# First recurrence of a hybrid decoder layer: scores packed as squares of 32 tokens

## The chip, the cores and the metric

The kernel runs on one core of a Trainium2 chip. A core has TensorE (matmul, with its own queue), VectorE (DVE), ScalarE (ACT), GpSimd (POOL) and a queue engine SyncE (SP) that only issues DMAs. The metric is the device time of one execution in microseconds.

## The reference

One decoder layer on 512 tokens of 1024 channels: a gated feed-forward part, a mixer with two recurrences, a second feed-forward part, each with a residual, and a last norm. All numbers are float32. The change touches the first recurrence (HGRN2, 8 heads of 128 channels):

```python
def hgrn2_chunked(q, k, v, log_f):
    """S_t = diag(f_t) S_{t-1} + k_t^T v_t (k_t = 1 - f_t), o_t = S_t^T q_t."""
    ...
        inter = jnp.einsum('bhtk,bhkv->bhtv', q_c * jnp.exp(b_c), S)
        diff = b_c[:, :, :, None, :] - b_c[:, :, None, :, :]
        decay = jnp.exp(jnp.where(causal, diff, -jnp.inf))
        scores = jnp.einsum('bhtk,bhsk,bhtsk->bhts', q_c, k_c, decay)
        intra = jnp.einsum('bhts,bhsv->bhtv', scores, v_c)
```

The score of a query token t and a key token s is a sum over channels of query, key and the product of all gates between s and t, zero for s > t.

## The kernel before

Matmul operands of the dense projections are split in two halves (a rounded `hi` and a rest `lo`), and `mm3` (lines 188 to 191) issues three matmuls per operand pair into one accumulator. The weights come in slabs of 512 columns through SP's queue; ScalarE casts the `hi` half (line 1754) and VectorE subtracts the `lo` half (line 1756), into three rotating pairs of buffers. The two feed-forward parts (`ffn`) stand before and after the mixer.

The mixer (`mixer`) has one thread (a Python generator) for each piece of work. A planner, `Desk` (lines 64 to 138), runs all threads in a simulated time and decides, engine by engine, in which order their instructions are recorded; the order on the chip is that order. A thread says `yield "use", engine, cost` before it issues (`V`, `A` and `T_`, lines 761 to 763, are the costs of VectorE, ScalarE and TensorE), `yield "get", tag, n` and `D.put` for places in a pool, `yield "on", event` and `D.fire` for events. The rank of a thread breaks ties. The thread `product` (rank 9) issues the dense projections in the order of `DENSE` and then `closing`, the projection of the second recurrence's output: 16 operand pairs `so[k]` for each of 8 output blocks, in quarters, those of blocks 0 and 1 taking turns.

The first recurrence is `h_head(i)`, one thread per head, in chunks of 128 tokens (`NT` = 4 of them). It never divides by a gate. It builds the 128 x 128 scores of a chunk, keys in partitions, queries in columns, by levels hh = 1, 2, 4 ... 64: at level hh the tokens form pairs of blocks of hh; the queries of a pair's second block meet the keys of its first one, after `qp` and `ke` were multiplied by the gates in between (line 988 on VectorE, `keys` at line 929 on GpSimd). Its steps, with their lines:

- 909 to 912: `qp` is the query times its gate; `qq` holds, per chunk, the 128 queries and beside them the 64 odd columns of `qp`.
- 913 to 920: the opening product `pd`: 4 matmuls, one per chunk, 128 keys against 192 columns, into two PSUM banks. Its diagonal is the score of a token with itself, and its last 64 columns are level 1.
- 921 to 925: the score tile `at` (name `ah`, two buffers of the pool `on`) gets the 128 columns of `pd` times the identity, so its diagonal and zeros elsewhere.
- 956 to 961: level 1, two masked copies (`copy_predicated` with the mask `hm`).
- 963 to 975: levels 2 to 16, `pl`: per chunk and square of 32 tokens one matmul of 32 keys against the 16 queries of second blocks, 16 matmuls per head and level. The two heads of a pair meet before each level ("at" events), so that their blocks stand together.
- 932 to 941 (`fill`): masked copies into the score tile, one for each of the four squares of 32 partitions, four per level.
- 942 to 946: levels 32 and 64 are copied by ScalarE.
- 1014 to 1037: `po`, scores times values plus queries times state, and the state's update, chunk after chunk.

The second recurrence (`g_e`, `g_n`, `g_b`, `g_inv`, `g_w`, `g_rec`, eight pairs of heads u) runs mostly after the first. Its triangular inverse starts on GpSimd (lines 1236 to 1241) from an identity that is loaded from `hmask` (line 1234). The outputs of the last pair, u = 7, go from two transposes (line 1445, `pto`) through VectorE (1449), ScalarE (1458) and VectorE (1460) into `so[14]` and `so[15]`, which the first quarter of `closing` that needs them reads.

Of the kernel before, what the change touches and what calls it, by code (L numbers as in the profile page):

```python
# [16 lines left out]
P = 128  # L17
T = 512
NT = T // P
# [118 lines left out]
        assert not self.asked, [(th.rank, th.want) for th in self.asked]  # L138


def body(tc, xT, cst, sqc, hmask, dta, w1o, w1a, w2a, wt, wn, wab, wbh, wbg, wo, w1b, w2b, yT, dbg=None):
    nc = tc.nc
    pe, act, dve, pool, sp = nc.tensor, nc.scalar, nc.vector, nc.gpsimd, nc.sync
    ctx = ExitStack()
# [12 lines left out]
    cs = cp.tile([P, 256], F32, name="cs")  # L157
    sq = cp.tile([P, 3, P], F32, name="sq")
    ident, tri, strict = sq[:, 0], sq[:, 1], sq[:, 2]
    hm = cp.tile([P, 5, 64], F32, name="hm")  # L160
    dtab = cp.tile([P, 32], F32, name="dtab")[:16, :2]
    ones = cp.tile([P, P], F32, name="ones")
    dve.memset(ones, 1.0)
# [451 lines left out]
        return pts, lambda: products(KD - 1, {1: spread})  # L615

    def lead():
        sp.dma_start(hm, hmask[:, 0:5])
        sp.dma_start(dtab, dta)

    def last(go, pl, units, on, hooks):
# [66 lines left out]
def mixer(tc, mp, e):  # L688
# [29 lines left out]

    places = {}
    for size, names in ((1024, "n2:2 gz:2 fs:1 ut:1"), (512, "kn:3 gm:1 qm:2 gb:2 ln:1 at:4 vb:4 t64:2 on:2"),  # L720
                        (256, "ft:1 tp:1 thg:2 x:1 we:1 s:3 w:1"), (128, "fm:1"), (64, "sm:4")):
        for it in names.split():
            n, b = it.split(":")
            places[n] = alloc(n, int(b))

    hv = h.rearrange("p (a b) t -> p a (b t)", a=4)
    eye4 = e["hmask"][:, 5:9].rearrange("p a (i c) -> p (a i) c", c=8)


    lb0, lb1 = cs[:, C_LB:C_LB + 8], cs[:, C_LB + 8:C_LB + 16]  # L730
# [26 lines left out]


    D = Desk(wx0=1, wx1=1, wx2=1, wx3=1, mm=2, a=2, b=2, d=1, e=1, ta=TA, tm=6, thg=1, raw=RB, w=WB, n2=2, gz=2, fs=1, ut=1, t=3, kn=3, gm=1,
             qm=2, gb=2, ln=1, mi=3, mt=3, at=4, vb=4, t64=2, on=2, ft=1, x=1, we=1, w_=1, s=3)  # L760
    V = lambda n: ("use", "DVE", 0.21 + 0.001 * n)
    A = lambda n: ("use", "ACT", 0.2 + 0.0009 * n)
    T_ = lambda n: ("use", "PE", n)
# [4 lines left out]
    def place(tag, name, shape, n):  # L768

        taken[tag] = taken.get(tag, 0) + 1  # L770
        if taken[tag] == n:
            D.fire(("free", tag))
        return places[tag](name, shape)
# [82 lines left out]
    def h_q(i, pt):  # L856
        yield "get", "ta", 2
        yield "on", "rbc"
        yield *V(512), 1
        qs = ta("qs")  # L860
        dve.tensor_tensor(qs, pt, rbc, op=ALU.mult)
        D.put("mm")
        yield A(512)
        th = ta("th")
        act.activation(th, qs, AF.Tanh, scale=0.5)
        tag = ("fs", "ut")[i % 2]
        yield "get", tag, 1
        yield V(512)
        qq = hq[i] = place(tag, "qq", (P, NT, 192), 4)
        dve.scalar_tensor_tensor(qq[:, :, :P], v3(th, NT), 1.0, v3(qs, NT), op0=ALU.add, op1=ALU.mult)  # L870
        D.put("ta", 2)
        D.fire(("Q", i))

# [28 lines left out]
    def h_head(i):  # L902
# [3 lines left out]
        yield "get", "gb", 1  # L906
        yield V(512)
        qp = place("gb", "qp", (P, T), 8)
        dve.tensor_tensor(v3(qp, NT), qq[:, :, :P], v3(f, NT), op=ALU.mult)
        q4 = qp.rearrange("p (c g b) -> p c g b", c=NT, b=2)  # L910
        yield V(256)
        dve.tensor_copy(qq[:, :, P:192], q4[:, :, :, 1])
        yield "get", ln_, 2
        yield T_(1.32)
        pd = [ps("pd", ln_), ps("pd2", ln_)]
        for c in range(NT):
            pe.matmul(pd[c // 2][:, (c % 2) * 192:(c % 2) * 192 + 192], ke[:, c * P:(c + 1) * P], qq[:, c],  # L917
                      start=True, stop=True)
        D.put(tag_q)
        D.fire(("pd", i))  # L920
        yield "get", "on", 1
        at = place("on", "ah", (P, NT, P), 8)
        for q in range(2):
            yield V(256)
            dve.tensor_tensor(at[:, 2 * q:2 * q + 2], v3(pd[q][:, :384], 2)[:, :, :P], mid(ident, 2), op=ALU.mult)

        def keys(li, kv, fv, hh):
            yield "use", "POOL", .88
# [2 lines left out]

        def fill(li, hh, pl_):
            if hh <= 16:
                a5 = at.rearrange("p c (r g two b) -> p c r g two b", r=4, two=2, b=hh)
                for r in range(4):
                    rows = slice(32 * r, 32 * r + 32)
                    yield V(60)
                    dve.copy_predicated(a5[rows, :, r, :, 1],
                                        v3(hm[rows, li, 16 * r:16 * r + 16].bitcast(I32), 16 // hh).unsqueeze(1)
                                        .to_broadcast([32, NT, 16 // hh, hh]),  # L940
                                        pl_[rows, :NT * 16].rearrange("p (c g b) -> p c g b", c=NT, b=hh))
            else:
                for b in range(64 // hh):
                    s0 = 2 * b * hh
                    yield A(4 * hh)
                    act.copy(at[s0:s0 + hh, :, s0 + hh:s0 + 2 * hh], v3(pl_[s0:s0 + hh, :NT * hh], NT))
            D.put(ln_)
            D.fire(("full", i, li))

        fl, held = f, "at"  # L950
        for li, hh in enumerate((1, 2, 4, 8, 16, 32, 64)):
            n2 = T // (2 * hh)
            av = at.rearrange("p c (g two b) -> p c g two b", two=2, b=hh)
            if li:
                yield "on", ("ke", i, li - 1)
            if hh == 1:
                for q in range(2):
                    yield V(240)
                    dve.copy_predicated(av[:, 2 * q:2 * q + 2, :, 1, 0], mid(hm[:, li].bitcast(I32), 2),
                                        v3(pd[q][:, :384], 2)[:, :, P:192])  # L960
                D.put(ln_, 2)
            else:
                yield "get", ln_, 1
                D.fire(("at", i, li))
                yield "on", ("at", i ^ 1, li)
                yield T_(.6 if hh <= 16 else .5)
                pl_ = ps("pl", ln_)
                if hh <= 16:

                    qv = qp.rearrange("p (c r g two b) -> p c r g two b", c=NT, r=4, two=2, b=hh)  # L970
                    for c in range(NT):
                        for r in range(4):
                            s0 = 32 * r
                            pe.matmul(pl_[s0:s0 + 32, c * 16:(c + 1) * 16], ke[:, c * P + s0:c * P + s0 + 32],  # L974
                                      qv[:, c, r, :, 1], start=True, stop=True)
                else:
                    for c in range(NT):
                        for b in range(64 // hh):
                            s0 = 2 * b * hh
                            pe.matmul(pl_[s0:s0 + hh, c * hh:(c + 1) * hh], ke[:, c * P + s0:c * P + s0 + hh],  # L980
                                      qp[:, c * P + s0 + hh:c * P + s0 + 2 * hh], start=True, stop=True)
                D.start((2, i, 1), fill(li, hh, pl_))
            fv = fl.rearrange("p (g two) -> p g two", two=2)
            qv = qp.rearrange("p (g two b) -> p g two b", two=2, b=hh)
            kv = ke.rearrange("p (g two b) -> p g two b", two=2, b=hh)
            D.start((2, i), keys(li, kv, fv, hh))
            yield V(270)
            dve.tensor_tensor(qv[:, :, 1], qv[:, :, 1], bc(fv[:, :, 0], hh), op=ALU.mult)
            tag = ("x", "we")[i % 2] if hh == 1 else ("w", "ft")[i % 2] if hh == 2 else "tm"
            yield "get", "w_" if tag == "w" else tag, 1  # L990
            yield V(min(n2, 200))
            fn = tm(f"fl{hh}", (P, n2)) if tag == "tm" else place(tag, f"fl{hh}", (P, n2), 4)
            dve.tensor_tensor(fn, fv[:, :, 0], fv[:, :, 1], op=ALU.mult)
            yield "on", ("ke", i, li)
            D.put(held)
            if hh == 1:
                D.fire(("L", i))
            fl, held = fn, "w_" if tag == "w" else tag
# [18 lines left out]
        for c in range(NT):  # L1017
# [5 lines left out]
            pe.matmul(o, at[:, c], v[:, c, hs], start=True, stop=c == 0)  # L1023
            if c > 0:
                pe.matmul(o, qp[:, c * P:(c + 1) * P], s, start=False, stop=True)
            if c < NT - 1:
                pu = ps("pu", "b")
                pe.matmul(pu[:, :P], kn[:, c], v[:, c, hs], start=True, stop=True)
# [829 lines left out]
    D.start((0,), norm())  # L1858
    D.start((3, -1), loader())
    D.start((9,), product())  # L1860
    for i in range(8):
        D.start((2, i), h_head(i))
    for i in range(4):
# [58 lines left out]
def layout(i):  # L1922
# [8 lines left out]
        conv.reshape(4, 32, P).transpose(2, 1, 0).reshape(P, 128)], axis=1)  # L1931
    a = np.arange(P)
    sqc = np.stack([np.eye(P), a[:, None] <= a[None, :], a[None, :] < a[:, None]], 1)
    hmask = np.zeros((P, 9, 64))
    for l, hh in enumerate(LEVELS):
        g, b = np.divmod(np.arange(64), hh)
        hmask[:, l] = (a[:, None] >= 2 * hh * g) & (a[:, None] < 2 * hh * g + hh)
    eye4 = np.eye(32).reshape(32, 8, 4).transpose(2, 0, 1)
    hmask[:, 5:] = np.tile(np.repeat(eye4, 8, axis=0), (4, 1, 1)).reshape(P, 4, 64)
    w_in = f["w_in"][0]  # L1940
    off = np.cumsum([0, 1024, 1024, 1024, 1024, 1024, 1024, 2048, 16, 16, 2048, 1024, 1024])
    part = [w_in[:, off[j]:off[j + 1]] for j in range(12)]
# [7 lines left out]
    def ffn(n):  # L1950
# [3 lines left out]
    w1a, w2a = ffn(1)  # L1954
    w1b, w2b = ffn(2)
    out = dict(
        xT=_kpn(x.T), cst=cst, sqc=sqc, hmask=hmask,
        dta=np.stack([f["gdn_dt_bias"][0], f["gdn_a_log"][0]], 1),
        w1o=w1a[ORDER[0]:ORDER[0] + 2].reshape(4, P, KD, P).transpose(2, 1, 0, 3).reshape(KD, P, 512),
        w1a=w1a, w2a=w2a, wt=wt, wn=wn, wab=_kpn(wab).reshape(P, -1),  # L1960
# [18 lines left out]
```

## Time and profile before

| | us |
|---|---|
| median of 3 runs | 1606.91 |
| lowest, highest run | 1606.55, 1606.93 |
| span of the profiled execution | 1604.7 |
| TensorE busy in it | 1593.7 |
| VectorE busy | 1145.7 |
| ScalarE busy | 831.0 |
| GpSimd busy | 408.8 |

The profile is of one execution; its span runs from the first to the last instruction, so the time of a run is a little longer. In its rows, PE is TensorE's matmul and PEld its weight load, L917 is line 917 of the kernel, `pd<-qq,ke` names the output and the inputs, `128*32` the rows and columns of the stationary operand, `128x48` would be the moving one. In a timeline the first two numbers are the start and the duration in us, and xN merges N instructions of a kind. An fp32 matmul appears as two passes (x8 for four matmuls), a transpose and the split ones as one. The duration of a matmul holds its way through the array, so consecutive ones overlap: the spacing of their starts is the time they cost.

### The profile page before, as it was taken

The numbers are of one execution on the slowest core, as the hardware profiler recorded it, in microseconds if no ns is written. First come the engines' busy times: TensorE is split into PE (matmuls) and PEld (weight loads), VectorE is DVE, ScalarE is ACT, GpSimd is POOL, SyncE is SP. The second block draws the span as 40 slices with busy tenths as digits, with TensorE's granted clock in tenths as the row PEclk, the third lists the DMA queues.
The fourth block names the chain that finished last, engine by engine and source line by source line (L and its number), as shares of the span: only waits on it lengthen the run. The fifth ranks groups of instructions, "written<-read, shape, count | busy, mean of one in ns | idle before, by whom it ended". The sixth has DMA issues, their size and how long they took to land.

```text
span 1604.7 us, 29242 instructions
## 1 busy us (share of the span) xinstructions
PE 1593.7 (99%) x10672; PEld 1386.3 (86%) x10672; DVE 1145.7 (71%) x2259; ACT 831.0 (52%) x1872; POOL 408.8 (25%) x725
## 2 busy tenths in 40 slices
PE   9999999999999999999999999999999999999997
PEld 8999998888888888888888888888888899999887
DVE  6888785447787778668788888765545788878433
ACT  5766674332434345456665665554324666667222
POOL 0211212001221221156545556600001121121001
PEclk9999999999999999999999999999999999999998
DMA  5766863332312322443242334445543586686333
GB/s 187 168 162 156 181 160 103 113 117 86 106 47 68 86 92 87 137 135 104 93 125 80 119 107 129 134 136 186 164 142 128 140 183 158 154 187 146 92 91 117
DMA packets 121824, 204.91 MB, mean 128 GB/s; under 512 B 21184, under 2 KB 27072, under 8 KB 121680
## 3 DMA queue, kind: packets, MB, share of 16 engines
q1 hardware_dynamic: 104688, 172.40, 34.3%
q0 software_dynamic: 14400, 26.22, 10.2%
q10 hardware_dynamic: 2592, 4.42, 1.0%
q8 instruction: 84, 1.38, 0.4%
q14 instruction: 60, 0.49, 0.1%
HBM read 188.02 MB, written 14.97 MB: 126 GB/s over the span
## 4 chain that ended last, share of the span: by engine, by line
PE 91%; DMA 3%; issue 3%; DVE 2%; ACT 0%; POOL 0%; POOLq 0%; SPq 0%; DVEq 0%; ACTq 0%
PE pmm L189 19%; PE pmm L191 19%; PE pmm L190 19%; PE px L191 6%; PE px L190 6%; PE px L189 6%; DMA wlo<-w1a 2%; PE pnat L189 2%; PE pnat L191 2%; PE pnat L190 2%; PE pgq L1189 1%; PE pw L1387 1%; PE pog L1403 1%; PE pl L974 1%; PE pd L917 1%
## 5 line engine op out<-in xcount | busy, mean ns | idle before, releaser
L189 PE MATMUL pmm<-uh,whi 128*128 128x512 f32 x879 | 361.3, 411 | 0.0
L191 PE MATMUL pmm<-uh,wlo 128*128 128x512 f32 x879 | 343.0, 390 | 0.0
L190 PE MATMUL pmm<-ul,whi 128*128 128x512 f32 x879 | 341.9, 389 | 0.0
L191 PE MATMUL px<-xs,wlo 128*128 128x256 f32 x1008 | 285.7, 283 | 1.3 <-DMA wlo<-w1a 0.7
L190 PE MATMUL px<-xs,whi 128*128 128x256 f32 x1008 | 285.2, 283 | 0.0
L189 PE MATMUL px<-xs,whi 128*128 128x256 f32 x1008 | 285.2, 283 | 0.0
L1754 ACT CAST whi<-raw 128x512 fp32r<-128x512 f32 x226 | 140.2, 621 | 242.7 <-PE pmm L190 195.2
L1756 DVE TENSOR_TENSOR wlo<-raw,whi 128x512 fp32r<-128x512 f32 x226 | 158.3, 702 | 118.2 <-ACT whi L1754 116.2
L191 PEld LDWEIGHTS pmm<-uh,wlo 128*128 128x128 f32 x879 | 165.0, 188 | 36.1 <-DVE wlo L607 0.2
L191 PEld LDWEIGHTS px<-xs,wlo 128*128 128x128 f32 x1008 | 193.5, 192 | 2.1 <-DMA wlo<-w1a 1.1
L189 PEld LDWEIGHTS px<-xs,whi 128*128 128x128 f32 x1008 | 193.5, 192 | 0.1
L190 PEld LDWEIGHTS px<-xs,whi 128*128 128x128 f32 x1008 | 193.5, 192 | 0.1
L189 PEld LDWEIGHTS pmm<-uh,whi 128*128 128x128 f32 x879 | 165.5, 188 | 30.4
L190 PEld LDWEIGHTS pmm<-ul,whi 128*128 128x128 f32 x879 | 165.7, 189 | 29.5 <-DVE ul L216 0.2
L329 ACT CAST whi<-sw 128x512 fp32r<-128x512 f32 x144 | 87.6, 613 | 92.8 <-DVE sw L366 72.6
L308 DVE TENSOR_TENSOR wlo<-raw,whi 128x512 fp32r<-128x512 f32 x100 | 77.7, 788 | 76.7 <-ACT whi L329 76.3
L329 ACT CAST whi<-raw 128x512 fp32r<-128x512 f32 x104 | 61.2, 592 | 125.6 <-PE pmm L190 92.8
L227 POOL TENSOR_TENSOR acc<-acc,sqt 128x512 f32<-128x512 f32 x18 | 23.4, 1302 | 319.8 <-ACT sqt L225 319.8
L308 DVE TENSOR_TENSOR wlo<-sw,whi 128x512 fp32r<-128x512 f32 x144 | 98.0, 681 | 0.0
L329 ACT CAST whi<-rw 128x512 fp32r<-128x512 f32 (+1 forms) x130 | 79.6, 613 | 26.6 <-PE px L190 13.4
L190 PE MATMUL pmm<-xs,whi 128*128 128x512 f32 (+1 forms) x238 | 89.7, 377 | 0.1
L189 PE MATMUL pmm<-xs,whi 128*128 128x512 f32 (+1 forms) x238 | 89.8, 377 | 0.0
(476 smaller groups left out, 3223.5 us busy)
## 6 DMA issues: line engine op xcount, KB each, us to landing
raw<-wt SPq DMA_DIRECT2D x160, 256.0 KB
rw<-w1b SPq DMA_DIRECT2D x80, 256.0 KB
rw<-w1a SPq DMA_DIRECT2D x74, 256.0 KB
wlo<-w1b POOLq DMA_DIRECT2D x53, 256.0 KB, 4.8
wlo<-w1a POOLq DMA_DIRECT2D x47, 256.0 KB, 5.0
raw<-w2b SPq DMA_DIRECT2D x41, 256.0 KB
raw<-w2a SPq DMA_DIRECT2D x36, 256.0 KB
raw<-wn SPq DMA_DIRECT2D x32, 256.0 KB
```

The source lines that it names most:

```text
L189: pe.matmul(pt, ah, bh, start=first, stop=False)
L190: pe.matmul(pt, ah, bl, start=False, stop=False)
L191: pe.matmul(pt, al, bh, start=False, stop=last)
L227: add.tensor_tensor(acc, acc, s, op=ALU.add)
L308: dve.tensor_tensor(lo, x, hi.bitcast(F32), op=ALU.subtract)
L329: act.copy(hi, x)
L917: pe.matmul(pd[c // 2][:, (c % 2) * 192:(c % 2) * 192 + 192], ke[:, c * P:(c + 1) * P], qq[:, c], start=True, stop=True)
L974: pe.matmul(pl_[s0:s0 + 32, c * 16:(c + 1) * 16], ke[:, c * P + s0:c * P + s0 + 32], qv[:, c, r, :, 1], start=True, stop=True)
L1189: pe.matmul(pq[:, (c % 2) * 256:(c % 2) * 256 + 256], kq[:, c, 0], kq[:, c].rearrange("p a b -> p (a b)"), start=True, stop=True)
L1387: pe.matmul(pw[:, hd2[i]], ut[:, 4 * i + c], xs[i], start=True, stop=True)
L1754: act.copy(hi, raw)
L1756: dve.tensor_tensor(lo, raw, hi.bitcast(F32), op=ALU.subtract)
```

## The change

The opening product is made per square of 32 tokens: 16 matmuls of 32 keys against 48 columns (the 32 queries of the square and its 16 odd columns), into one PSUM bank, each square of 32 in its own 32 output partitions. The scores up to level 16 stay in a packed tile `ac` (128 x 4 x 32), which starts as `pd` times an identity of 32 and takes each level in one masked copy. At level 16 four copies on ScalarE put the four squares in place in the score tile. There are two score tiles in all, `ah`, made once and set to zero once by GpSimd; the copies of head i wait until the last product of head i - 2 has been issued (event "po"). The planner's costs go with it: 0.7 for the opening product (1.32 before), one V(128) for the identity (two V(256)), one V(64) per level (two V(240), four V(60)), four A(128). The mask array shrinks to 7 x 16 columns per partition, and the identity for the triangular inverse becomes an input of its own.

```diff
-    hm = cp.tile([P, 5, 64], F32, name="hm")
+    hm = cp.tile([P, 7, 16], F32, name="hm")
...
-        sp.dma_start(hm, hmask[:, 0:5])
+        sp.dma_start(hm, hmask)
...
-                        (256, "ft:1 tp:1 thg:2 x:1 we:1 s:3 w:1"), (128, "fm:1"), (64, "sm:4")):
+                        (256, "ft:1 tp:1 thg:2 x:1 we:1 s:3 w:1"), (128, "fm:1 ac:2"), (64, "sm:4")):
...
-    eye4 = e["hmask"][:, 5:9].rearrange("p a (i c) -> p (a i) c", c=8)
+    eye4 = e["eye4"].rearrange("p (i c) -> p i c", c=8)
+    eye32 = hm[:, 5:7].rearrange("p a b -> p (a b)")
...
-        qq = hq[i] = place(tag, "qq", (P, NT, 192), 4)
-        dve.scalar_tensor_tensor(qq[:, :, :P], v3(th, NT), 1.0, v3(qs, NT), op0=ALU.add, op1=ALU.mult)
+        qq = hq[i] = place(tag, "qq", (P, 16, 48), 4)
+        dve.scalar_tensor_tensor(qq[:, :, :32], v3(th, 16), 1.0, v3(qs, 16), op0=ALU.add, op1=ALU.mult)
...
-        dve.tensor_tensor(v3(qp, NT), qq[:, :, :P], v3(f, NT), op=ALU.mult)
-        q4 = qp.rearrange("p (c g b) -> p c g b", c=NT, b=2)
+        dve.tensor_tensor(v3(qp, 16), qq[:, :, :32], v3(f, 16), op=ALU.mult)
         yield V(256)
-        dve.tensor_copy(qq[:, :, P:192], q4[:, :, :, 1])
-        yield "get", ln_, 2
-        yield T_(1.32)
-        pd = [ps("pd", ln_), ps("pd2", ln_)]
+        dve.tensor_copy(qq[:, :, 32:], qp.rearrange("p (k g two) -> p k g two", k=16, two=2)[:, :, :, 1])
+        yield "get", ln_, 1
+        yield T_(.7)
+        pd = ps("pd", ln_)
         for c in range(NT):
-            pe.matmul(pd[c // 2][:, (c % 2) * 192:(c % 2) * 192 + 192], ke[:, c * P:(c + 1) * P], qq[:, c],
-                      start=True, stop=True)
+            for r in range(4):
+                s0 = 32 * r
+                pe.matmul(pd[s0:s0 + 32, c * 48:(c + 1) * 48], ke[:, c * P + s0:c * P + s0 + 32], qq[:, 4 * c + r],
+                          start=True, stop=True)
+        pd = v3(pd[:, :192], NT)
         D.put(tag_q)
         D.fire(("pd", i))
+        yield "get", "ac", 1
+        ac = places["ac"]("ac", (P, NT, 32))
+        yield V(128)
+        dve.tensor_tensor(ac, pd[:, :, :32], mid(eye32, NT), op=ALU.mult)
         yield "get", "on", 1
-        at = place("on", "ah", (P, NT, P), 8)
-        for q in range(2):
-            yield V(256)
-            dve.tensor_tensor(at[:, 2 * q:2 * q + 2], v3(pd[q][:, :384], 2)[:, :, :P], mid(ident, 2), op=ALU.mult)
+        yield "on", *([("po", i - 2)] if i > 1 else ["zero"])
+        at = ah[i % 2]
...
             if hh <= 16:
-                a5 = at.rearrange("p c (r g two b) -> p c r g two b", r=4, two=2, b=hh)
-                for r in range(4):
-                    rows = slice(32 * r, 32 * r + 32)
-                    yield V(60)
-                    dve.copy_predicated(a5[rows, :, r, :, 1],
-                                        v3(hm[rows, li, 16 * r:16 * r + 16].bitcast(I32), 16 // hh).unsqueeze(1)
-                                        .to_broadcast([32, NT, 16 // hh, hh]),
-                                        pl_[rows, :NT * 16].rearrange("p (c g b) -> p c g b", c=NT, b=hh))
+                yield V(64)
+                dve.copy_predicated(ac.rearrange("p c (g two b) -> p c g two b", two=2, b=hh)[:, :, :, 1],
+                                    v3(hm[:, li].bitcast(I32), 16 // hh).unsqueeze(1).to_broadcast([P, NT, 16 // hh, hh]),
+                                    pl_[:, :NT * 16].rearrange("p (c g b) -> p c g b", c=NT, b=hh))
+                if hh == 16:
+                    for r in range(4):
+                        s0 = 32 * r
+                        yield A(128)
+                        act.copy(at[s0:s0 + 32, :, s0:s0 + 32], ac[s0:s0 + 32])
+                    D.put("ac")
...
             if hh == 1:
-                for q in range(2):
-                    yield V(240)
-                    dve.copy_predicated(av[:, 2 * q:2 * q + 2, :, 1, 0], mid(hm[:, li].bitcast(I32), 2),
-                                        v3(pd[q][:, :384], 2)[:, :, P:192])
-                D.put(ln_, 2)
+                yield V(64)
+                dve.copy_predicated(ac.rearrange("p c (g two) -> p c g two", two=2)[:, :, :, 1],
+                                    mid(hm[:, li].bitcast(I32), NT), pd[:, :, 32:])
+                D.put(ln_)
...
+            if c == NT - 1:
+                D.fire(("po", i))
...
+    ah = [places["on"]("ah", (P, NT, P)) for _ in range(2)]
+
+    def zero():
+        for x in ah:
+            yield "use", "POOL", 1.0
+            pool.memset(x, 0.0)
+        D.fire("zero")
+    D.start((2,), zero())
```

More of the change, by code (lines that the diff above doesn't have):

```diff
@@ L138, in run, with body @@
         assert not self.asked, [(th.rank, th.want) for th in self.asked]
-def body(tc, xT, cst, sqc, hmask, dta, w1o, w1a, w2a, wt, wn, wab, wbh, wbg, wo, w1b, w2b, yT, dbg=None):
+def body(tc, xT, cst, sqc, hmask, eye4, dta, w1o, w1a, w2a, wt, wn, wab, wbh, wbg, wo, w1b, w2b, yT, dbg=None):
     nc = tc.nc
@@ L759, in mixer @@
     D = Desk(wx0=1, wx1=1, wx2=1, wx3=1, mm=2, a=2, b=2, d=1, e=1, ta=TA, tm=6, thg=1, raw=RB, w=WB, n2=2, gz=2, fs=1, ut=1, t=3, kn=3, gm=1,
-             qm=2, gb=2, ln=1, mi=3, mt=3, at=4, vb=4, t64=2, on=2, ft=1, x=1, we=1, w_=1, s=3)
+             qm=2, gb=2, ln=1, mi=3, mt=3, at=4, vb=4, t64=2, on=2, ft=1, x=1, ac=2, we=1, w_=1, s=3)
     V = lambda n: ("use", "DVE", 0.21 + 0.001 * n)
@@ L952, in h_head @@
             n2 = T // (2 * hh)
-            av = at.rearrange("p c (g two b) -> p c g two b", two=2, b=hh)
             if li:
@@ L1933, in layout @@
     sqc = np.stack([np.eye(P), a[:, None] <= a[None, :], a[None, :] < a[:, None]], 1)
-    hmask = np.zeros((P, 9, 64))
+    hmask = np.zeros((P, 7, 16))
+    s = a[:, None] % 32
     for l, hh in enumerate(LEVELS):
-        g, b = np.divmod(np.arange(64), hh)
-        hmask[:, l] = (a[:, None] >= 2 * hh * g) & (a[:, None] < 2 * hh * g + hh)
+        g = np.arange(16) // hh
+        hmask[:, l] = (s >= 2 * hh * g) & (s < 2 * hh * g + hh)
+    hmask[:, 5:] = (s == np.arange(32)).reshape(P, 2, 16)
     eye4 = np.eye(32).reshape(32, 8, 4).transpose(2, 0, 1)
-    hmask[:, 5:] = np.tile(np.repeat(eye4, 8, axis=0), (4, 1, 1)).reshape(P, 4, 64)
+    eye4 = np.tile(np.repeat(eye4, 8, axis=0), (4, 1, 1)).reshape(P, 256)
     w_in = f["w_in"][0]
@@ L1956, in layout @@
     out = dict(
-        xT=_kpn(x.T), cst=cst, sqc=sqc, hmask=hmask,
+        xT=_kpn(x.T), cst=cst, sqc=sqc, hmask=hmask, eye4=eye4,
         dta=np.stack([f["gdn_dt_bias"][0], f["gdn_a_log"][0]], 1),
```

## The prediction

> **What bounds the kernel now.** I read the page first, then the waits of TensorE, then the stage in which the changed lines run (the first lines of that work start at 377 us, the last end near 640 us), and there the timeline matmul by matmul.
>
> ```profile
> span 1604.7 us, 29242 instructions
> ...
> PE 1593.7 (99%) x10672; PEld 1386.3 (86%) x10672; DVE 1145.7 (71%) x2259; ACT 831.0 (52%) x1872; POOL 408.8 (25%) x725
> ...
> PE   9999999999999999999999999999999999999997
> ```
>
> ```profile
> PE pbc L654 <- POOL rl L252: 1.1, 1, 1.1
> PE pwarm L588 <- DVE mhalf L165: 1.1, 1, 1.1
> PE pst L648 <- ACT p L641: 0.8, 1, 0.8
> PE px L191 <- DMA wlo<-w1a: 0.7, 2, 0.5
> PE px L191 <- DMA wlo<-w1b: 0.4, 1, 0.4
> ```
>
> ```profile
> 377.00:640.00 263.00, 263.00 (x2407) 217.48 (x2406) 206.41 (x532) 109.14 (x275) 57.17 (x69) 1.00 0.26 79
> ```
>
> The first fence says that TensorE is busy in every slice. The second lists all of its waits (us in total, times, longest): 4.1 us in the whole span, at its two ends and in the two feed-forward parts, none on a line of the mixer. The third is the stage (PE, PEld, DVE, ACT, POOL busy): PE 263.00 of 263.00 us at full clock, VectorE 206.4, ScalarE 109.1. So the mixer lasts as long as the list of TensorE's instructions, and a change there is worth what it takes from or adds to that list, plus any wait it creates. "Busy" hides waits shorter than a matmul's own tail, so I also looked at the spacing of the dense matmuls: it is 0.227 us everywhere in the rows below, except beside small matmuls.
>
> **Part 1: the opening product.** Before, one head issues 4 matmuls `ke` (128 columns) against `qq` (192 columns). Each fp32 matmul is two passes in the trace, so 8:
>
> ```profile
> 377.57 0.39 PE L191 MATMUL pmm<-uh,wlo 128*128 128x512 f32 x1
> 377.80 1.46 PE L917 MATMUL pd<-qq,ke 128*128 128x192 f32 x8
> 378.96 0.53 PE L189 MATMUL pmm<-uh,whi 128*128 128x512 f32 x1
> 379.33 0.40 PE L190 MATMUL pmm<-ul,whi 128*128 128x512 f32 x1
> ```
>
> From 377.57 to 379.33 are 1.76 us; without the block two dense steps of 0.227 would lie there. The block costs 1.306 us, 0.163 per pass. After, a head issues 16 matmuls of 32 stationary and 48 moving columns, 32 passes. The columns streamed are the same, 8 x 192 = 32 x 48 = 1536. All the gain there can be is that the four groups of 32 output partitions work at once. The kernel already has such blocks, the level products, two heads in a row each:
>
> ```profile
> 392.44 0.39 PE L191 MATMUL pnat<-wx,ul 128*128 128x512 f32 x1
> 392.75 0.74 PE L974 MATMUL pl<-qp,ke 128*32 128x16 f32 x64
> 393.42 0.49 PE L189 MATMUL pnat<-whi,uh 128*128 128x512 f32 x1
> 393.75 0.39 PE L190 MATMUL pnat<-wlo,uh 128*128 128x512 f32 x1
> ```
>
> ```profile
> 412.02 0.70 PE L980 MATMUL pl<-qp,ke 128*32 128x32 f32 x32
> 412.65 0.50 PE L189 MATMUL pmm<-uh,whi 128*128 128x512 f32 x1
> ...
> 415.60 1.15 PE L980 MATMUL pl<-qp,ke 128*64 128x64 f32 x16
> 416.67 0.50 PE L189 MATMUL pmm<-uh,whi 128*128 128x512 f32 x1
> ```
>
> ```profile
> L974 PE MATMUL pl<-qp,ke 128*32 128x16 f32 x1024 | 11.8, 185 | 0.0
> ...
> L980 PE MATMUL pl<-qp,ke 128*64 128x64 f32 x64 | 4.6, 225 | 0.0
> L980 PE MATMUL pl<-qp,ke 128*32 128x32 f32 x128 | 2.8, 197 | 0.0
> ```
>
> A block's duration less that of its last pass is the spread of its starts. 16 columns, four groups: 0.74 - 0.185 = 0.555 us over 63 steps, 8.8 ns a pass, 35 ns a round of four. 32 columns, two groups: 0.70 - 0.197 = 0.503 over 31, 16.2 ns a pass, 32 ns a round. 64 columns, one group: 0.925 over 15, 62 ns. Streaming alone takes 0.163 x 16/192 = 13.6 ns for 16 columns, so four of them (54 ns) lie in a round of 35, and two of 32 (54 ns) in 32: groups do overlap, at least 1.5 to 1.7 fold. Entry and exit: 392.75 comes 0.31 after the matmul before it (0.08 over a dense step), the next dense one follows the last small start by 0.67 - 0.555 = 0.115 (0.145 in the block of 64 columns), and the one after it by 0.33 (0.10 over). Together 0.30 to 0.33 us per block.
>
> For 48 columns in four groups, full overlap gives a round between the 32 ns of 32 columns and the 62 of 64; the plain streaming time is 41 ns. I take 45. Eight rounds: 7 x 45 + 3 x 6 = 0.333 us, with entry and exit of 0.335 it is 0.67 per head. The gain is 1.306 - 0.67 = 0.636 us, times 8 heads 5.1 us. Bounds: rounds of 35 ns (the 16-column row) give 0.60 and 5.6 us. If no more than the shown 1.7 passes overlap, a round takes 4 x 41 / 1.7 = 96 ns, the block 1.03, the gain 2.2 us. With no overlap 32 x 41 ns + 0.335 = 1.65 us, a loss of 2.7 us. I choose the first, because the 16-column block keeps four weight loads and four streams going in one round and nothing in its row shows that it is the streams that fill it: its round is as long as that of two 32-column groups.
>
> One rule of the Trainium skill speaks against this: "TensorE: Matmul & The Clock Gate", section "Wait — 56ns, not 53.3ns?", says that matmuls never start closer than about 25 ns apart, however few columns they have. By it 31 steps would take at least 0.78 us, the block 1.11 and the gain would be 1.6 us. The 8.8 ns between passes of different groups contradict it for this form, so I do not sum by it.
>
> **Part 2: the packed scores on VectorE, ScalarE, GpSimd and the queues.**
>
> ```profile
> L938 DVE COPY_PREDICATED ah<-hm,pl 32x64 f32<-32x64 int32 x128 | 31.0, 242 | 3.1
> ...
> L925 DVE TENSOR_TENSOR ah<-pd,sq 128x256 f32<-128x256 f32 x16 | 6.3, 417 | 2.2 <-PE pd L917 2.1
> L959 DVE COPY_PREDICATED ah<-hm,pd 128x128 f32<-128x128 int32 x16 | 5.8, 464 | 0.0
> ```
>
> ```profile
> L1278 ACT COPY gt<-gtp 32x128 f32<-32x128 f32 x16 | 4.7, 295 | 0.2
> ```
>
> ```profile
> ACT whi L1754 <- PE pmm L190: 28.4, 22, 3.0
> ```
>
> VectorE loses 31.0 + 6.3 + 5.8 = 43.1 us. It gets, per head, one product of 128 columns (between 0.242 and 0.417) and five masked copies of 64 columns (0.242 for 64 columns of 32 partitions, at most the 0.464 of 128 columns): 1.5 to 2.7 us, near the lower end because 64 columns are 64 columns; some 13 us in all. The net 30 us are counted as nothing: no matmul of the mixer waited for VectorE. ScalarE gets four copies per head, 4 x 0.295 x 8 = 9.4 us in a stage where it has 154 us free. A copy of them can wait for the masked copy of 16 tokens or for the last product of the head before the last (new order "po"); behind it in ScalarE's queue stand the weight casts of L1754, for which TensorE's slabs wait. These casts are early: their idle time ended 22 times on TensorE giving a buffer back, each slab feeds 12 dense matmuls (2.7 us), and three pairs of buffers rotate. With two slabs in hand some 4 us cover such a wait; without that cover the copies would cost their wait one for one. I count nothing.
>
> ```profile
> L1633 POOL MEMSET gut<- 128x1024 f32 x1 | 1.0, 956 | 4.8 <-PE pd L917 4.8
> ```
>
> ```profile
> 355.76 0.39 PE L191 MATMUL pmm<-roomb,wlo 128*128 128x512 f32 x1
> ```
>
> ```profile
> 361.12 1.42 POOL L1844 TENSOR_TENSOR rcol<-rcol,mhalf 128x4 f32<-128x4 f32 x1 [16.49 <-DVE rcol L1841]
> ```
>
> The two new memsets (512 columns, half of 0.956 each) stand on GpSimd directly before the `pow` of L1844, on which all scaling of the mixer waits. They must wait until the feed-forward buffers below them are free, whose last matmul ends at 356.15; GpSimd idles 16.49 us until 361.12, so they fit. Without that gap they would cost 1 us once. On SP's queue the mask load shrinks (128 x 112 instead of 128 x 320 numbers) and the eight 128 x 256 identity loads only change their source: nothing.
>
> **Part 3: the order.** The recorded order of the built programs shows what else moves. Stretches of small matmuls between dense ones are 208 instead of 209, so there is nothing in switching. But the second recurrence's last head (u = 7) does not come earlier by as much as the rest: its second transpose (L1445, `pto`) was followed by 36 dense matmuls before the first one that reads what comes out of it (operand pair k = 15 of output block 0); now 9 lie between.
>
> ```profile
> 1123.11 0.60 PE L1445 MATMUL pto<-sq,on 128*128 128x128 f32 x4
> ...
> 1123.46 0.48 PE L189 MATMUL pmm<-sop,whi 128*128 128x512 f32 x1
> ...
> 1123.74 0.75 DVE L1449 SCALAR_TENSOR_TENSOR on<-pto,cs,ggz 128x512 f32<-128x512 f32 x1 [0.15 <-PE pto L1445]
> ...
> 1124.73 0.62 ACT L1458 CAST uh<-on 128x512 fp32r<-128x512 f32 x1
> ...
> 1125.47 0.69 DVE L1460 TENSOR_TENSOR ul<-on,uh 128x512 fp32r<-128x512 f32 x1
> ```
>
> From the first transpose to `uh` are 2.24 us (1125.35), to `ul` 3.05 (1126.16). In the new order the 9 matmuls start 0.35 to 2.27 us after the transpose, the tenth (needs `uh`) at 2.49, the eleventh (needs `ul`) would at 2.72. TensorE then waits some 0.4 us; if ScalarE or VectorE is taken by a slab just then, 0.6 or 0.7 more each, 1.7 at most; if both answer at once, 0.1.
>
> **The sum.** -5.1 + 0.4 = -4.7 us. The profiled execution has a span of 1604.7; the runs shown take 1606.55 to 1606.93, median 1606.91, so about 2.2 us lie around the span, which the change does not touch. Span 1600.0, time **1602.2**.
>
> **The rivals.**
> - *Pairs, not fours.* The moving streams of the groups share what they are read through, and 1.7 at once, as both level rows show, is all there is. Block 1.03, gain 2.2 - 0.4 = 1.8: 1605.1; with an overlap of 1.5 the round is 109 ns, the block 1.12, and the time 1605.8. For it: no row shows more overlap of streams. Against: a round of four with 16 columns is not longer than one of two with 32. By the rule of the Trainium skill named above, passes 25 ns apart, the time would be 1605.7, and its chance is in this rival's.
> - *Slower: no overlap at 48 columns.* Place: the eight blocks. The streams run one after another, as many columns as before, plus entry and exit: 1.65 us, +2.7 + 0.4: 1610.0. It decides from a spacing of (1.306 - 0.335) / 31 = 31 ns per pass upwards. Against it stand 8.8 and 16.2 ns.
> - *The gain is given back at the end.* The second recurrence's chain through GpSimd and ScalarE sets when k = 14 and 15 come. If it does not move at all, TensorE reaches them 4.7 us early and waits: 1606.9. Against it: the first `pto` still has 84 rows of dense work (it had 81) before it after the last `pog`.
> - *The change does not do what it says:* VectorE's 30 us do nothing, as counted; this is inside the forecast.
>
> **How the numbers follow.** Forecast 0.70, own range 1600.9 (rounds of 35 ns, stall 0.1, another half us from order) to 1603.6 (stall 1.7). Pairs 0.14, no overlap 0.05, given back 0.11. A measurement of this kernel tells 0.2%, 3.2 us, from no change; faster is below 1603.7. Forecast and a little of the third make 0.72 faster; pairs and most of "given back" 0.21 same; no overlap and a longer wait 0.07 slower. The range reaches to the upper figure of the pairs, 1600.9 to 1605.8.
>
> **What would show it.** In the profile of after: 256 passes of `pd` with 128x48 in eight blocks of some 0.53 us duration (starts spread over 0.33), the next dense matmul 0.45 after the block's first start; PE x10864; a VectorE total near 1116 us; and one new line in TensorE's waits, `pmm` on the `ul` or `uh` of the last head, 0.1 to 1.7 us. The forecast is wrong if the spread is over 0.6 us, or if waits of TensorE on VectorE, ScalarE or slabs appear in the stage.

## The result and the profile after

The changed kernel takes **1609.75 us** (median of 11 runs, 1607.65 to 1611.29) against 1606.62 us for the kernel before in 11 runs beside it (1605.27 to 1607.59): ratio 1.0021, 95% interval 1.0012 to 1.0030. It is slower by 0.2%, 3.1 us, where 4.7 us less was forecast.

The page of the kernel after, its first lines:

```profile
span 1607.3 us, 29554 instructions
...
PE 1595.9 (99%) x10864; PEld 1379.2 (86%) x10864; DVE 1118.5 (70%) x2147; ACT 842.7 (52%) x1904; POOL 409.4 (25%) x727
```

TensorE's waits of the kernel after (us in total, times, longest):

```profile
PE pbc L654 <- POOL rl L252: 1.1, 1, 1.1
PE pwarm L588 <- DVE mhalf L165: 1.1, 1, 1.1
PE pmm L190 <- DVE ul L1550: 1.0, 1, 1.0
PE pst L648 <- ACT p L641: 0.8, 1, 0.8
PE px L191 <- DMA wlo<-w1b: 0.5, 1, 0.5
```

The timeline of TensorE in the kernel after, one opening product (start, duration), and under it the group of all eight (busy us, mean ns of one):

```profile
378.24 0.40 PE L191 MATMUL pmm<-uh,wlo 128*128 128x512 f32 x1
378.57 0.55 PE L919 MATMUL pd<-qq,ke 128*32 128x48 f32 x32
379.05 0.51 PE L189 MATMUL pmm<-uh,whi 128*128 128x512 f32 x1
379.39 0.40 PE L190 MATMUL pmm<-ul,whi 128*128 128x512 f32 x1
```

```profile
L919 PE MATMUL pd<-qq,ke 128*32 128x48 f32 x256 | 4.4, 209 | 0.0
```

As announced: 256 passes, PE x10864, VectorE down from 1145.7 to 1118.5 us. The block costs 379.39 - 378.24 - 2 x 0.227 = 0.70 us instead of 1.306 (six of the other seven 0.68 to 0.69; one stands behind other small matmuls). One wait of 1.0 us is new. A gain of 0.6 us per head and a wait of 1 us don't make a kernel slower by 3 us, so the time went elsewhere. TensorE's timeline shows where the stages begin: the first norm product of the mixer, of the second feed-forward part and of the last norm, before and then after:

```profile
358.70 0.28 PE L1837 MATMUL pst<-ones,acc 128*128 128x1 f32 x2
...
1246.66 0.28 PE L236 MATMUL pst<-ones,acc 128*128 128x1 f32 x2
...
1587.44 0.28 PE L646 MATMUL pst<-ones,acc 128*128 128x1 f32 x2
```

```profile
359.28 0.28 PE L1844 MATMUL pst<-ones,acc 128*128 128x1 f32 x2
...
1248.21 0.28 PE L236 MATMUL pst<-ones,acc 128*128 128x1 f32 x2
...
1590.42 0.28 PE L646 MATMUL pst<-ones,acc 128*128 128x1 f32 x2
```

The mixer takes 888.93 us after and took 887.96 before, although its eight blocks are 5 us shorter. The second feed-forward part, which the diff doesn't touch, takes longer too: from the second row to the third are 340.78 us before and 342.21 after. And at 12 us, long before any changed line, the distance between dense matmuls has already changed. First and last row of the same stretch, 14 steps in each; before, then after:

```profile
11.74 0.39 PE L190 MATMUL pmm<-ul,whi 128*128 128x512 f32 x1
...
14.91 0.39 PE L189 MATMUL pmm<-uh,whi 128*128 128x512 f32 x1
```

```profile
11.67 0.40 PE L190 MATMUL pmm<-ul,whi 128*128 128x512 f32 x1
...
14.93 0.40 PE L189 MATMUL pmm<-uh,whi 128*128 128x512 f32 x1
```

Before, 3.17 / 14 = 0.2264 us from start to start; after, 3.26 / 14 = 0.2329. The instructions of this stretch are the same, in the same order, and the granted clock is 0.997 in the profiled execution of the kernel before and 0.998 in that of the kernel after. "PE busy" is 99% in both, and no wait stands in the list: only the spacing shows it. It isn't everywhere. Near the end of the second feed-forward part of the kernel after, the same weights meet two kinds of moving tile:

```profile
1559.76 0.39 PE L189 MATMUL pmm<-xs,whi 128*128 128x512 f32 x1
...
1561.80 0.39 PE L189 MATMUL pmm<-roomb,whi 128*128 128x512 f32 x1
...
1562.48 0.40 PE L189 MATMUL pmm<-uh,whi 128*128 128x512 f32 x1
...
1563.18 0.40 PE L189 MATMUL pmm<-roomb,whi 128*128 128x512 f32 x1
...
1564.57 0.40 PE L189 MATMUL pmm<-uh,whi 128*128 128x512 f32 x1
```

From 1559.76 to 1562.48 are 12 steps, 0.2267 each; the three `uh`/`ul` matmuls that follow take 0.70, 0.2333 each. The spacing doesn't fall back at once: the six `roomb` matmuls behind them take 1.39 us, 0.2317 each. So not every slow step belongs to the tile that moves in it.

What differs is an address, as the order and the sizes of the allocations give it. The tile `hm` (L160) shrank from 5 x 64 to 7 x 16 numbers: 320 - 112 = 208 columns, 832 bytes per partition. All tiles made after it (`ones`, the weight slabs `whi`/`wlo`, `raw`, `xs`, the rooms of the mixer) start 832 bytes lower; those made ahead of it (`h`, `uh`, `ul`) stay. 832 is no multiple of 256 or 512, so the distance between a moving `uh` and its weights changed, while `xs` and the weights moved together.

The new wait, in the kernel after's timeline:

```profile
1128.59 0.60 PE L1452 MATMUL pto<-sq,on 128*128 128x128 f32 x4
1128.60 0.62 ACT L1761 CAST whi<-raw 128x512 fp32r<-128x512 f32 x1 [2.22 <-PE pmm L190]
...
1129.12 0.62 ACT L1548 CAST uh<-og 128x512 fp32r<-128x512 f32 x1
1129.25 0.69 DVE L1763 TENSOR_TENSOR wlo<-raw,whi 128x512 fp32r<-128x512 f32 x1 [2.15 <-ACT whi L1761]
1129.79 0.51 PE L189 MATMUL pmm<-uh,whi 128*128 128x512 f32 x1
1129.86 0.74 DVE L1456 SCALAR_TENSOR_TENSOR on<-pto,cs,ggz 128x512 f32<-128x512 f32 x1
1130.52 0.68 DVE L1550 TENSOR_TENSOR ul<-og,uh 128x512 fp32r<-128x512 f32 x1
1131.26 0.50 PE L190 MATMUL pmm<-ul,whi 128*128 128x512 f32 x1 [0.96 <-DVE ul L1550]
```

From 1129.79 to 1131.26 are 1.47 us where a dense step is 0.23: a stall of 1.24 us. The instruction that is late is L1550, which makes the rest `ul` of a block read back from memory (k = 13). It stands on VectorE's queue behind two others. The first is the subtraction of a weight slab (L1763), for which VectorE sat idle 2.15 us until ScalarE had cast the slab (L1761); that cast had itself waited 2.22 us for TensorE. The second is L1456, the reader of the last transposes (1128.59), which here starts without a wait of its own. The cast that L1550 needs (L1548) stands behind L1761 on ScalarE in the same way.

### The profile page after: what moved, and what is told of

It reads as the page before. It is cut to its first block, busy times and chain, and to the rows that moved or that the text cites. A ratio compares the mean times of both kernels' runs of the same rounds, so it can differ in the third digit from the quotient of the medians.

```text
span 1607.3 us, 29554 instructions
## 1 busy us (share of the span) xinstructions
PE 1595.9 (99%) x10864; PEld 1379.2 (86%) x10864; DVE 1118.5 (70%) x2147; ACT 842.7 (52%) x1904; POOL 409.4 (25%) x727
## 3 DMA queue, kind: packets, MB, share of 16 engines
q8 instruction: 85, 1.39, 0.4%
## 4 chain that ended last, share of the span: by engine, by line
PE 90%; DMA 5%; issue 4%; POOL 0%; DVE 0%; ACT 0%; POOLq 0%; SPq 0%; ACTq 0%
PE pmm L189 20%; PE pmm L191 19%; PE pmm L190 19%; PE px L191 5%; PE px L190 5%; PE px L189 5%; DMA wlo<-w1a 2%; DMA wlo<-w1b 2%; PE pnat L189 2%; PE pnat L190 2%; PE pnat L191 2%; PE pgq L1196 1%; PE pw L1394 1%; PE pog L1410 1%; PE pl L979 1%
## 5 line engine op out<-in xcount | busy, mean ns | idle before, releaser
L1761 ACT CAST whi<-raw 128x512 fp32r<-128x512 f32 x226 | 140.1, 621 | 234.1 <-PE pmm L190 204.2
L1763 DVE TENSOR_TENSOR wlo<-raw,whi 128x512 fp32r<-128x512 f32 x226 | 158.6, 702 | 139.5 <-ACT whi L1761 130.7
```

What stands on the lines that cost most here:

```text
L1761: act.copy(hi, raw)
L1763: dve.tensor_tensor(lo, raw, hi.bitcast(F32), op=ALU.subtract)
```

## The experiments

Two theories. **A**: the shift of 832 bytes makes the dense matmuls slower whose moving tile stayed while the weights moved. **B**: the addresses don't matter, and the loss comes from the new instructions and their order. The kernels of experiments 1, 2, 6 and 7 ran together, with 27 runs of the kernel before beside them (median 1606.31); those of 3 to 5 and 8 ran together, with 14 (median 1606.72).

**1. The changed kernel with the old room for `hm`** (`a_pad`). Same instructions, same order, old addresses:

```diff
-    hm = cp.tile([P, 7, 16], F32, name="hm")
+    hm = cp.tile([P, 320], F32, name="hm")[:, :112].rearrange("p (a b) -> p a b", a=7)
```

> The changed kernel with one line different: the mask tile hm is given 320 columns of room again (as before the change) and uses the first 112, so every tile behind it in SBUF starts 832 bytes later, where it started before, counted modulo 512 bytes. Every engine has the same instructions in the same order as the changed kernel. Theory A (addresses: dense matmuls whose weight tile and moving tile start at different offsets modulo 512 bytes are 3 to 5 ns slower, some 2400 of them): the spacing of dense matmuls with uh or ul moving in the opening 60 us goes back from 232 to 227 ns, the time to about 1606.6 - 5.1 (opening product) + 1.2 (the wait at the end) = 1602.7 us. Theory B (the new order, the extra ScalarE copies or the extra instructions slow TensorE): spacing and time stay at the changed kernel's, 1609.7 us.

Measured: 1604.3 us (1602.77 to 1606.01, 11 runs), ratio 0.9988 (0.9980 to 0.9997). The stretch shown above (14 steps, 3.17 us, 0.2264 each):

```profile
11.65 0.39 PE L191 MATMUL pmm<-uh,wlo 128*128 128x512 f32 x1
...
14.82 0.39 PE L190 MATMUL pmm<-ul,whi 128*128 128x512 f32 x1
```

One line that changes no instruction turns 3.1 us lost into 2.0 us won. B falls for these 5.1 us. The stall at L1550 stays (1.0 us in the list of waits), so it belongs to the order and not to the addresses.

**2. The kernel before, shifted** (`b_shift192`): 48 columns more, 192 bytes, which leaves the weights at the same place modulo 512 as in the changed kernel.

```diff
-    hm = cp.tile([P, 5, 64], F32, name="hm")
+    hm = cp.tile([P, 368], F32, name="hm")[:, :320].rearrange("p (a b) -> p a b", a=5)
```

> The kernel before, with the same instructions in the same order, but hm given 368 columns of room instead of 320 (48 unused), so that every tile behind it starts 192 bytes later, the same offset modulo 512 as in the changed kernel. Theory A: dense matmuls with uh or ul moving slow by 3 to 5 ns, time about 1606.6 + 7.7 = 1614.3 us. Theory B: nothing happens, 1606.6 us.

Measured: 1611.61 us (1611.26 to 1612.11, 5 runs), ratio 1.0033 (1.0020 to 1.0046): 5.3 us lost without any part of the change. A's direction is right, its price of 7.7 us too high; the next experiments give the price. The stretch of before here has 16 steps in 3.66 us, 0.2288 each:

```profile
11.30 0.39 PE L189 MATMUL pmm<-uh,whi 128*128 128x512 f32 x1
...
14.96 0.39 PE L190 MATMUL pmm<-ul,whi 128*128 128x512 f32 x1
```

That is slower than 0.2264, but not the 0.2329 of the kernel after, although the distance of the operands is the same modulo 512. The distance alone doesn't fix a spacing; what else does isn't shown.

**3 to 5. Three more rooms** (`a_off256`, `a_off128`, `a_off64`): the changed kernel with 128, 160 and 336 columns for `hm`, one run each.

```diff
-    hm = cp.tile([P, 7, 16], F32, name="hm")
+    hm = cp.tile([P, 128], F32, name="hm")[:, :112].rearrange("p (a b) -> p a b", a=7)
```

> The changed kernel with 128 columns of room for hm: the weight tiles start 256 bytes off the moving tiles uh and ul, modulo 512. Same instructions in the same order. If only offsets that are no multiple of 128 bytes cost, the dense matmuls with uh or ul moving in the opening 60 us are at 227 ns as in a_pad; if whole rows of 512 bytes count, at 230 to 233 as in the changed kernel. Theory B (not addresses): as the changed kernel.

> The same with 160 columns of room: weight tiles 384 bytes off the moving tiles modulo 512, that is 128 modulo 256. 227 ns if a multiple of 128 bytes is enough, over 230 if 256 or 512 are needed.

> The same with 336 columns of room: 64 bytes off modulo 512 (the changed kernel is 192 off, which is 64 modulo 128). If 128 bytes are the period, this is as slow as the changed kernel, 230 to 233 ns in the opening 60 us; if 64 bytes are enough, 227.

Measured: 1603.64, 1613.66 and 1616.53 us, beside 1606.72 for the kernel before. The stretch of before, in the kernel with 128 columns (14 steps, 3.17 us) and in the one with 336 (13 steps, 3.04 us, 0.2338 each):

```profile
11.70 0.39 PE L189 MATMUL pmm<-uh,whi 128*128 128x512 f32 x1
...
14.87 0.39 PE L191 MATMUL pmm<-uh,wlo 128*128 128x512 f32 x1
```

```profile
11.80 0.40 PE L189 MATMUL pmm<-uh,whi 128*128 128x512 f32 x1
...
14.84 0.39 PE L190 MATMUL pmm<-ul,whi 128*128 128x512 f32 x1
```

For all seven kernels I took every pair of consecutive dense matmuls of 512 columns with dense ones beside them and under 0.29 us from start to start, and sorted them by the start of the moving tile less the start of the weights, in bytes modulo 512. Mean ns (count):

| kernel | 0 | 64 | 128 | 192 | 256 | 320 | 384 | 448 |
|---|---|---|---|---|---|---|---|---|
| before | 228.0 (4042) | | | | | | | |
| after | 227.6 (1439) | | | 233.2 (328) | | 230.0 (2266) | | |
| room 320 | 228.1 (4040) | | | | | | | |
| before, shifted | 227.7 (1434) | | | 233.1 (336) | | 229.8 (2265) | | |
| room 128 | 226.9 (1439) | | | | 228.7 (2595) | | | |
| room 160 | 227.3 (1439) | | 232.5 (2267) | | | | 232.7 (328) | |
| room 336 | 227.3 (1439) | 229.6 (328) | | | | | | 233.3 (2266) |

(A handful of pairs at a change of tile were left out. The median of the 256 column is 227, as in the 0 column; its mean is 1.8 ns higher, but the same matmuls have it in the kernel before too, 228.7 against 226.9.) Columns 256 apart agree: 0 and 256; 64 and 320; 128 and 384; 192 and 448. So what counts, as far as these four values tell, is the distance **modulo 256 bytes**. Against the 228.0 of the kernel before, 64 costs some 2 ns in the mean, 128 some 4.5, 192 some 5. The 0 column of the shifted kernels holds tiles that moved together with the weights: it's the distance between the two operands, not where either starts. The columns 64 and 192 also show that the sign matters: with the roles swapped (`pnat`, where the slab streams and `uh` is the weights) 328 matmuls lie at the opposite distance and pay the opposite price.

The means hide where the cost falls. After a break, such as a block of small matmuls, the spacing is uneven in all seven kernels: the first three steps of `uh` and `ul` matmuls take 231 to 234 ns in the mean, whatever the distance. From the eleventh step on (some 1,000 pairs in each kernel) it has settled: at 226.7 ns in the three kernels at a multiple of 256, at 229.4 and 229.7 in the two at 320, at 232.7 at 128 and at 233.3 at 448. So long dense stretches pay most, and the short ones between the mixer's small matmuls little.

The price for the kernel after: its mean over all counted pairs is 229.40 (the row above weighted), before's is 228.02; 1.38 ns x 4039 = **5.6 us**. For the shifted kernel before the same gives 5.3 us, which is what it lost. For the rooms of 128, 160 and 336 columns it gives 0.2, 10.7 and 11.5 us; against `a_pad`, each beside its own runs of before, the single runs lost -1.1, 9.0 and 11.8.

**6. The pair of k = 15 later** (`a_pad_tail`), meant to remove the stall: on top of the old room, the closing product takes k = 15 of the output blocks 0 and 1 after k = 12 to 14 of both.

```diff
...
+            if q == 3 and d < 2:
+                if d == 0:
+                    for e_, js in ((0, (0, 1, 2)), (1, (0, 1, 2)), (0, (3,)), (1, (3,))):
+                        yield from some(e_, q, js)
...
+                continue
...
```

> As a_pad, and in the closing projection operand pair k = 15 of output blocks 0 and 1 is taken after pairs 12 to 14 of both, so that 18 dense matmuls instead of 9 stand between the last transposes and the first matmul that reads what they lead to. If the wait of 1.0 us on the last subtraction (pmm L190 <- DVE ul) is real loss, it vanishes and the time is a_pad's less 1.2: 1601.5 us by theory A, 1608.5 by theory B. If the loss only moves, the time stays a_pad's.

Measured: 1606.13 us (1604.85 to 1606.75), ratio 0.9996 (0.9988 to 1.0005): a miss, 1.8 us worse than without it. Of its waits:

```profile
PE pmm L189 <- DVE mg L1583: 1.1, 1, 1.1
...
PE pmm L190 <- DVE ul L1550: 1.0, 1, 1.0
PE po L1030 <- DVE hs L1041: 0.9, 1, 0.9
```

The wait at L1550 didn't move, since it belongs to k = 13. Both accumulators now end together, and the next block waits for L1583 to empty them. The third row is a stall at 424 us, far from the edit: there a weight slab's DMA kept ScalarE waiting 2.21 us, and VectorE's work behind that cast came late. Whether other executions had this too, one profile doesn't tell.

**7. The opening product as before** (`a_pad_wide`), the rest of the change kept, on the old room: four products of 128 x 192, and the squares taken out of them by small VectorE operations.

```diff
...
-            for r in range(4):
-                s0 = 32 * r
-                pe.matmul(pd[s0:s0 + 32, c * 48:(c + 1) * 48], ke[:, c * P + s0:c * P + s0 + 32], qq[:, 4 * c + r],
-                          start=True, stop=True)
+            pe.matmul(pd[c // 2][:, (c % 2) * 192:(c % 2) * 192 + 192], ke[:, c * P:(c + 1) * P], qq[:, c],
+                      start=True, stop=True)
...
```

> As a_pad, but the opening product is issued as before the change: 4 matmuls of 128 keys against 192 columns per head into two banks, with the packed squares taken out of it in quarters by VectorE (16 small instructions per head instead of 2). If the product per square is worth what its rows say (1.306 - 0.67 us per head), the time is a_pad's plus 5.1 us: 1607.8 by theory A, 1614.8 by theory B. If the squares' product gains nothing in the end, it equals a_pad.

Measured: 1608.42 us (1607.85 to 1609.0), ratio 1.0011 (1.0002 to 1.0020), 4.1 us above `a_pad`. Its first block:

```profile
376.87 0.39 PE L191 MATMUL pmm<-uh,wlo 128*128 128x512 f32 x1
377.10 1.46 PE L918 MATMUL pd<-qq,ke 128*128 128x192 f32 x8
378.27 0.53 PE L189 MATMUL pmm<-uh,whi 128*128 128x512 f32 x1
378.63 0.40 PE L190 MATMUL pmm<-ul,whi 128*128 128x512 f32 x1
```

378.63 - 376.87 - 2 x 0.227 = 1.31 us, as before; in `a_pad` the same working gives 379.96 - 378.83 - 2 x 0.227 = 0.68. The opening product per square is worth 8 x (1.31 - 0.68) = 5.0 us by the rows, seen as 4.1 in the time. What makes up the 0.9 between isn't shown. The list of waits has less at the read-back line, here L1557, than the 1.0 of `a_pad`, with 0.2 more at L1474:

```profile
PE pmm L190 <- DVE ul L1557: 0.3, 1, 0.3
```

By the starts these two steps together lose 1.09 us (0.59 and 0.50) and the one of `a_pad` 1.23, so the stall at the end explains little of it. VectorE has 1141.3 us of work here, nearly as much as before (1145.7), so this run doesn't tell what its relief alone is worth.

**8. The read-back earlier** (`a_pad_back5`): on the old room, the planner may convert a block read back 5 us after its DMA instead of 6.

```diff
-LAG = dict(raw=3.5, gb=6.5, nb=6, m=7, out=5, back=6)
+LAG = dict(raw=3.5, gb=6.5, nb=6, m=7, out=5, back=5)
```

> As a_pad with the planner's delay for a spilled output that is read back set to 5 us instead of 6. On VectorE the subtractions of the read-back pairs (ul of L1550) then stand before the scaling of the last transposes (L1456), for which they stood waiting, and 24 dense matmuls of the last quarters' lower pairs stand behind the last transposes. If the wait pmm L190 <- DVE ul L1550 of 1.0 us is that queue order, it goes, and the time is a_pad's less 1.2 us: 1603.1. If the pair's data itself is late from DRAM, the wait stays and the time too, 1604.3.

Measured: **1602.89 us** (1601.56 to 1605.75, 10 runs) against 1606.72, ratio 0.9977 (0.9967 to 0.9986). VectorE's timeline at the last transposes:

```profile
1123.24 0.69 DVE L1550 TENSOR_TENSOR ul<-og,uh 128x512 fp32r<-128x512 f32 x1
1124.57 0.75 DVE L1456 SCALAR_TENSOR_TENSOR on<-pto,cs,ggz 128x512 f32<-128x512 f32 x1 [0.64 <-PE pto L1452]
1125.74 0.69 DVE L1763 TENSOR_TENSOR wlo<-raw,whi 128x512 fp32r<-128x512 f32 x1 [0.41 <-ACT whi L1761]
```

All of its waits on TensorE:

```profile
PE pbc L654 <- POOL rl L252: 1.1, 1, 1.1
PE pwarm L588 <- DVE mhalf L165: 1.1, 1, 1.1
PE pst L648 <- ACT p L641: 0.8, 1, 0.8
PE px L191 <- DMA wlo<-w1a: 0.4, 1, 0.4
PE px L191 <- DMA wlo<-w1b: 0.3, 1, 0.3
```

L1550 stands ahead of L1456 and of a slab's subtraction (L1763), and the wait is gone; the run moved it ahead of both, so it doesn't tell which of them cost more. This version beats both kernels. Against `a_pad` it gains 1.8 us, each beside its own runs of before; the two intervals overlap, so here the list of waits is the stronger evidence.

## Why the prediction was wrong

**The step that failed** is the sentence of Part 2 on SP's queue: the mask load shrinks, "nothing". The load was looked at, the tile was not. Its size sets where all later tiles start; 832 bytes less put some 2,600 dense matmuls off the distance at which they run at 0.227 us, and that cost 5.6 us by the spacings of the profiles, 5.1 by the runs (`a_pad` against the kernel after, each beside its own runs of before). Without this the change gains 2.0 us (`a_pad`), which lies in the range but is less than half of the 4.7 forecast; with the last stall mended it gains 3.8.

**Part 1 was right.** Block 0.67 forecast, 0.68 (`a_pad`) and 0.70 measured; spread of the starts 0.33 forecast, 0.55 - 0.209 = 0.34 measured. The choice of four groups at once over 1.7 held, so the rivals "pairs, not fours" (1.03) and "no overlap" (1.65) fall. Those 31 steps are 11 ns each on average. The rule of the Trainium skill in "TensorE: Matmul & The Clock Gate", section "Wait — 56ns, not 53.3ns?", that starts are never closer than some 25 ns, doesn't hold in this block, whose passes go to four column groups; the prediction had the same from the level products.

**The rest of Part 2 was right in its sum.** VectorE fell by 27.2 us (30 forecast), and no wait of TensorE on VectorE, ScalarE or a slab appeared in the stage of the first recurrence. Nor did VectorE's relief bring anything of its own: the mixer of `a_pad` (norm products at 359.96 and 1244.97 us) is 2.95 us shorter than before's, less than the 5.0 of its blocks. Of the cover, one number was wrong, here and in the description of the kernel before: six pairs of weight buffers rotate (`WB`), not three.

**Part 3 had the place, but the wrong instruction and size.** A wait at the last head's transposes came, 1.24 us where 0.4 stood, within its bounds of 0.1 to 1.7. I followed the operand pair that comes out of the transposes (k = 15). What was late was the pair of k = 13, whose data need no transpose: on VectorE it only stands behind a slab's subtraction and the transposes' reader. That a slab can take ScalarE or VectorE just then was in the bounds; that the pair in front is hit by it was not. `a_pad_tail`, built on the same reading, missed for that reason; `a_pad_back5` moved the right instruction and the wait went.

**"The gain is given back at the end"** is true of 1.24 us of it, not of all. **"No overlap at 48 columns"** gave 1610.0, only 0.25 us off the measured time, and that is luck: its block of 1.65 us didn't come. The measured 3.1 us lay outside the range because no rival held a loss outside the changed stage.

The terms against the forecast, with the distance as the runs give it: 5.1 (distance of the operands) + 0.8 (stall) + 0.2 (blocks) + 0.3 = 6.4 of the 7.8 us between forecast and result. The 0.3 is a step of 0.49 us at 814.45 us of the kernel after, where TensorE's next weight load waited for VectorE (`zg`, L1501); the kernel before has no such step there. The other 1.4 us are not traced. The runs of one kernel here lie up to 4.2 us apart, and the first feed-forward part, whose matmuls are the same, took 358.70 us in the profile of before, 359.96 in `a_pad` and 358.16 in the kernel with 128 columns.

## What to carry to other kernels

When a change resizes a tile, all tiles made after it move: before costing the change, work out by how many bytes, and compare the spacing of untouched matmuls in a stretch far from it. Keep moving tiles and weight tiles that meet in long dense stretches at starts that are equal modulo 256 bytes, and give a resized tile its old room as a control with the same instructions. And on an engine's queue ask not only who waits for a result, but which ready work stands behind the instruction that waits.

## What the runs showed of the hardware

The mean spacing of dense 128 x 512 matmuls goes with the distance between the starts of the moving tile and the weight tile within a partition, modulo 256 bytes: 227 to 229 ns at 0, 230 at 64, 232.5 at 128, 233 at 192, in four kernels off the old distance and three on it, at granted clocks of 0.997 to 0.998. At 0 the spacing settles to 226.7 ns some ten steps after a break; at the other distances it stays above. Neither busy shares nor waits show it. Which of the two reads is delayed, the stream or the load of the next weights, wasn't tried, nor distances other than multiples of 64. Matmuls of 256 columns show no such difference where `uh` and `roomb` alternate in the kernel after (0.119 us a step from 1586.48 to 1587.91 us).
